# Hybrid encoder block: tile addresses, first norm weights, low parts and opening order

## Chip, cores and metric

One core of a Trainium2 chip (trn2) runs the whole block. The metric is device time in microseconds of one execution; the kernel before took 1340.28 us in the median of three runs (1338.75 to 1340.47).

## What is computed

The reference is one encoder layer on 512 tokens of width 1024, all in float32:

```python
h = rmsnorm(x, g_pre_ffn1)
x = x + 0.5 * rmsnorm(swiglu(h, w_gu1, w_down1), g_post_ffn1)
h = rmsnorm(x, g_pre_mix)
qa, ka, va, qd, kd, vd, ga, gb = split(h @ w_in)
oa = differential_attention(rope(qa), rope(ka), va)   # 8 heads
od = dilated_attention(rope(qd), rope(kd), vd)        # 3 groups of 4 heads
merged = sigmoid(ga) * (oa @ w_proj_a) + sigmoid(gb) * (od @ w_proj_b)
x = x + rmsnorm(merged @ w_out, g_post_mix)
h = rmsnorm(x, g_pre_ffn2)
x = x + 0.5 * rmsnorm(swiglu(h, w_gu2, w_down2), g_post_ffn2)
```

`swiglu` splits `h @ w_gu` into two halves of 2816 columns and returns `(silu(g) * u) @ w_down`.

## The kernel before

**Products in three parts.** Every large float32 operand is split into a high part (a cast to fp32r on ScalarE, L75) and a low part (source minus high part, L76, on VectorE or, where a call names it, on GpSimd). `mm3` (L78 to L81) makes each product of three fp32r matmuls, high by high (L79), high by low (L80) and low by high (L81). Activations lie transposed: `xth`/`xtl` hold the normed input of a stage, `hth`/`htl` the hidden layer of a feed-forward, `odh`/`odl` and `oah`/`oal` the two mixers' outputs, `mh`/`ml` the merged ones.

**Stages.** Feed-forward 1 (`f1`), the mixers, feed-forward 2 (`f2`). In `ffn`, eleven steps of 256 hidden columns make `f1a`/`f2a` from weights (stationary) and `xth`/`xtl` (moving, 512 tokens); the first step does tokens 0 to 255 for all its weights and then tokens 256 to 511. `natural_out` makes the down product with `hth`/`htl` slices as stationary and 512 columns of weights as moving operand, in two halves (`f1dy`, `f1dz`). In its second half the last four weight units are gone through token tile by token tile, and after each tile come the post norm, the residual and the next stage's `pre_norm`, so that the next stage can begin.

**`pre_norm(j, g)`** (L169): two squares with sums on ScalarE, a few 128x1 instructions on VectorE, two `xn` products on VectorE (L179), eight transposes on TensorE (L183), and the split of the result into `xth` (ScalarE) and `xtl` (VectorE).

**Low parts on GpSimd.** The four weight units of the first step of each feed-forward (`f1g`, `f2g` with `fp == 0`, L251), those of `vd0`, the first projection of the mixers (L304), and, left as they are by the change, most query and key units and the first gates.

**Opening** (L792 to L813): 14 warm-up matmuls on the identity, the load of `x` and of three weight units, and `gain(..., on_chip=True)`, which loads one row of 1024 norm weights by ScalarE's queue and spreads it over 128 partitions with a GpSimd instruction (L102). The first `pre_norm` needs it in L179.

**Order.** The framework orders the instructions of every engine itself, by a simulated timeline, from the program order and the dependences; each engine then runs its list in that order.

**Addresses.** Pools are laid one behind the other: `cp` (identity, `xs`, `xth`, `xtl`, norm weights), `wp` (weights), `sp` (small tiles, `xn`, temporaries), then the stage pools (`hp` with `hth`/`htl`; `mp`, `vp`, `op`, `bp`, `dp`). A small tile takes 32 bytes of a partition. By the allocations of this program `cp` and `wp` lie at multiples of 64 bytes (and 128 past a multiple of 256); the odd number of small tiles in `sp` puts `hth`, `htl`, `odh`, `odl`, `oah`, `oal`, `va`, `vd`, the score operands, `xn` and the temporaries 32 bytes past a multiple of 64, and `mh`, `ml`, counted from the other end, as well.

Of the kernel before, what the change touches and what calls it, by code (L numbers as in the profile page):

```python
# [2 lines left out]

# [1 line left out]

# [6 lines left out]
F32 = mybir.dt.float32  # L12
F32R = mybir.dt.float32r
# [5 lines left out]
P = 128  # L19
# [7 lines left out]
ROPE_THETA = 500000.0  # L27
ROT = 16
LAMBDA_INIT = 0.8 - 0.6 * math.exp(-0.3 * 0)
WARM = 14  # L30
SCALE = 1.0 / math.sqrt(64)
NEG = -1e30
C_QA, C_KA, C_VA, C_QD, C_KD, C_VD, C_GA, C_GB = 0, 1024, 2048, 3072, 3840, 4608, 5376, 6400
# [3 lines left out]
def kernel(  # L37
# [8 lines left out]
    nc = tc.nc  # L46
# [4 lines left out]
    w_in = w_in[0]  # L51
# [4 lines left out]
    cp = ctx.enter_context(tc.tile_pool(name="cp", bufs=1))  # L56
    wp = ctx.enter_context(tc.tile_pool(name="wp", bufs=4))
    sp = ctx.enter_context(tc.tile_pool(name="sp", bufs=4))
    ps = ctx.enter_context(tc.tile_pool(name="ps", bufs=4, space=bass.MemoryType.PSUM))

    ident = cp.tile([P, P], F32, name="ident")
    make_identity(nc, ident)
    xs = cp.tile([P, NT, D], F32, name="xs")
# [3 lines left out]
    def psum1(name):  # L67
        return ps.tile([P, 512], F32, tag="p", name=name, bufs=4)
# [4 lines left out]
    def split(hi, lo, src, eng=None):  # L73

        nc.scalar.copy(hi, src)  # L75
        (eng or nc.vector).tensor_tensor(out=lo, in0=src, in1=hi.bitcast(F32), op=ALU.subtract)  # L76
# [11 lines left out]
    def wsplit(raw, a, b, name, eng=None, pool=None):  # L88
        hi = (pool or wp).tile([P, a, b], F32R, tag="wh", name=f"{name}_h")
        lo = (pool or wp).tile([P, a, b], F32R, tag="wl", name=f"{name}_l")  # L90
        split(hi[:], lo[:], raw[:], eng)
        return hi, lo

    def wunit(src, a, b, name, eng=None, pool=None):

        return wsplit(wload(src, a, b, name), a, b, name, eng, pool)

    def gain(g, tag, on_chip=False):
        t = cp.tile([P, D], F32, tag=tag, name=tag)
        if on_chip:  # L100
            nc.scalar.dma_start(t[0:1, :], g)
            nc.gpsimd.partition_broadcast(t[:], t[0:1, :])  # L102
        else:
            nc.sync.dma_start(t[:], g.broadcast_to([P, D]))
        return t

    def small(n, name, dt=F32):
        return sp.tile([P, n], dt, tag=f"{name}{n}", name=name, bufs=1 if name[:2] in ("ys", "pi", "pf", "ld") else 2 if n == 1 else 3)

    def newton(eng, v, r, n):  # L110

# [134 lines left out]
    def ffn_units(w_gu, tag, fp):  # L246

        def block(m, kh):
            c0 = m * FF + fp * 256
            name = f"{tag}g{fp}_{m}{kh}"  # L250
            eng = nc.gpsimd if fp == 0 else None  # L251
            return (lambda: wload(w_gu[kh * 512:(kh + 1) * 512, c0:c0 + 256], 4, 256, name),
                    lambda raw: wsplit(raw, 4, 256, name, eng))
        return [block(m, kh) for m in range(2) for kh in range(2)]

    def ffn(w_gu, w_down, tag, post, after, first=None):
# [23 lines left out]
    def mixers(mix):  # L280
        mp = mix.enter_context(tc.tile_pool(name="mp", bufs=1, reuse_waits="tile"))
# [1 line left out]
        odl = mp.tile([P, 2, S], F32R, name="odl")  # L283
        cosT = mp.tile([P, S], F32, name="cosT")
        sinT = mp.tile([P, S], F32, name="sinT")
        gsub = mp.tile([P, 1], F32, name="gsub")
        nc.sync.dma_start(gsub[:], g_subln.rearrange("a e -> e a"))
        nlam = mp.tile([P, 1], F32, name="nlam")

        def tmp(name, dt=F32):  # L290
            return sp.tile([P, 512], dt, tag="t", name=name, bufs=6)
# [2 lines left out]
        def vproj(c0, cols, put, tag):  # L294
            nu = 8 * cols // 1024
            kk = ND // nu
            us = []

            accs = {}

            def token_half(j, h):
                if not us:
                    us.extend(wunit(w_in[u * kk * P:(u + 1) * kk * P, c0:c0 + cols], kk, cols, f"{tag}{u}",
                                    nc.gpsimd if tag == "vd0" else None) for u in range(nu))  # L304
                if h == 0:
                    accs[j] = psum1(f"{tag}a{j}")
                acc = accs[j]
                for u in range(h * nu // 2, (h + 1) * nu // 2):
                    wh, wl = us[u]
                    for i in range(kk):  # L310
                        k = u * kk + i
                        c = slice(j * P, (j + 1) * P)
                        mm3(acc[:, :cols], xth[:, k, c], xtl[:, k, c], wh[:, i, :], wl[:, i, :], k == 0, k == ND - 1)
                if h == 1:
                    nc.scalar.copy(put(j), acc[:, :cols])
            return [lambda j=j, h=h: token_half(j, h) for j in range(NT) for h in range(2)]


        def rope_tables(bp):
            n = NT * 8  # L320
            scratch = tmp("rt")

            def piece(i):
                return scratch[:, i * n:(i + 1) * n]

            pi = small(NT, "pi", I32)
            nc.sync.dma_start(pi[:], positions.rearrange("b (p j) -> p (b j)", j=NT))
            fr = piece(0)
            nc.sync.dma_start(fr, inv_freq)
            pf = small(NT, "pf")  # L330
            nc.vector.tensor_copy(pf[:], pi[:])
            ang = piece(1)
            nc.vector.tensor_tensor(
                out=ang.rearrange("p (j f) -> p j f", j=NT), in0=fr.rearrange("p (j f) -> p j f", j=NT),
                in1=pf[:].unsqueeze(2).broadcast_to([P, NT, 8]), op=ALU.mult)

            a1 = bp.tile([P, n], F32R, name="a1")
            a2 = piece(2)
            split(a1[:], a2, ang)
            parts, rest = [], 1.0 / (2.0 * math.pi)  # L340
            for _ in range(4):
                e = math.floor(math.log2(rest)) - 11
                b = math.floor(rest / 2.0 ** e) * 2.0 ** e
                parts.append(b)
                rest -= b
            magic = 1.5 * 2.0 ** 23

            def less_round(dst, src):

                t = piece(3)  # L350
                nc.vector.tensor_scalar(t, src, magic, None, op0=ALU.add)
                nc.vector.scalar_tensor_tensor(
                    out=dst, in0=t, scalar=magic, in1=src, op0=ALU.subtract, op1=ALU.subtract)

            u = piece(4)
            nc.vector.memset(u, 0.0)
            for a, m in ((a2, 3), (a1[:].bitcast(F32), 4)):
                for b in reversed(parts[:m]):
                    w = piece(5)
                    nc.vector.tensor_scalar(w, a, b, None, op0=ALU.mult)  # L360
                    less_round(w, w)
                    nc.vector.tensor_tensor(out=u, in0=u, in1=w, op=ALU.subtract)
            for dst, shift in ((sinT, 0.0), (cosT, 0.25)):
                v = piece(6 if shift else 7)
                nc.vector.tensor_scalar(v, u, shift, None, op0=ALU.add)
                less_round(v, v)
                t = piece(8 if shift else 9)
                nc.scalar.activation(t, v, AF.Sin, scale=-6.2831850)
                wide = tmp("wide")
                nc.vector.memset(wide[:], shift * 4.0)  # L370
                wv = wide[:].rearrange("p (j c d) -> p j c d", j=NT, c=2)
                tv = t.rearrange("p (j f) -> p j f", j=NT)
                for c in range(2):
                    if shift == 0.0:
                        nc.vector.tensor_scalar(wv[:, :, c, 0:8], tv, -1.0, None, op0=ALU.mult)
                    else:
                        nc.vector.tensor_copy(wv[:, :, c, 0:8], tv)
# [346 lines left out]
        ep = mix.enter_context(tc.tile_pool(name="ep", bufs=1, side="right", reuse_waits="tile"))  # L724
        mh = [vp.tile([P, 4, S], F32R, tag="v", name="mh0"), ep.tile([P, 4, S], F32R, name="mh1")]
        ml = ep.tile([P, ND, S], F32R, name="ml")

        def pieces(w, c0, nk, a, tag):
            us = [wunit(w[u * 512:min(nk * P, (u + 1) * 512), c0:c0 + 256], min(4, nk), 256, f"{tag}{u}")
# [11 lines left out]
        with tc.tile_pool(name="gp", bufs=1, reuse_waits="tile") as gp:  # L741
# [4 lines left out]
            for cp_ in range(4):  # L746
                c0 = cp_ * 256
# [32 lines left out]
        for j in range(NT):  # L780
            c = slice(j * P, (j + 1) * P)
# [15 lines left out]
    nc.scalar.activation(one[:], one[:], AF.Sqrt)  # L797
    nc.sync.dma_start(xs[:, 0, :], x_v[:, 0, :])
    nc.sync.dma_start(xs[:, 1, :], x_v[:, 1, :])
    g_pre = gain(g_pre_ffn1, "gpre", on_chip=True)  # L800
    steps = ffn_units(w_gu1, "f1", 0)
    raws = [ld() for ld, _ in steps[:3]]
    for j in range(2, NT):
        nc.sync.dma_start(xs[:, j, :], x_v[:, j, :])
    pre_norm(0, g_pre)
    pre_norm(1, g_pre)
    first = [sp_(r) for (_, sp_), r in zip(steps, raws)]
    first.append(steps[3][1](steps[3][0]()))
    pre_norm(2, g_pre)
    pre_norm(3, g_pre)  # L810
    post1 = Post(gain(g_post_ffn1, "gpost"), 0.5)
    g_pre2 = gain(g_pre_mix, "gpre")
    ffn(w_gu1, w_down1, "f1", post1, lambda j: pre_norm(j, g_pre2), first)  # L813
# [48 lines left out]
```

## Time and profile before

| | |
|---|---|
| median of three runs | 1340.28 us |
| the profiled execution | 1340.15 us |
| its span, first to last instruction | 1338.3 us |
| TensorE busy | 1308.1 us (98%) |
| VectorE, ScalarE, GpSimd busy | 611.9, 507.6, 207.9 us |
| mean granted TensorE clock | 0.988 |

The profiled execution lies 0.13 us under the median, with 1.85 us outside its span. TensorE's busy time counts overlapping matmuls once, so the distance from one matmul's start to the next says more than its duration.

### The profile page before, as it was taken

The page shows a single profiled execution, that of the slowest core. Times are in us where ns is not written, and L with a number is a line of the kernel's source. Part 1 is how long each engine was busy: PE and PEld are TensorE (multiplying, and loading weights), DVE is VectorE, ACT ScalarE, POOL GpSimd, SP SyncE. Part 2 cuts the span into 40 slices and gives each one's busy share as a digit, 9 for nine tenths or more (in the row PEclk, how much of TensorE's full clock was granted, in tenths as well). Part 3 has the DMA queues.
Part 4 walks back from the last instruction along what each step waited for, and adds up shares of the span by engine and source line. Part 5 has one row for each costly group of instructions (what it writes and reads, how often), then busy time and mean ns, then how long its engine had stood idle before and what let it go on. Part 6 is the DMA issues. An engine that isn't in the chain of part 4 may idle for free.

```text
span 1338.3 us, 15865 instructions
## 1 busy us (share of the span) xinstructions
PE 1308.1 (98%) x6304; PEld 1077.1 (80%) x6304; DVE 611.9 (46%) x1046; ACT 507.6 (38%) x869; POOL 207.9 (16%) x209
## 2 busy tenths in 40 slices
PE   6999999999999999999999999999999999999997
PEld 6988888888878877887777788888798888888886
DVE  6333333323265265428889944435843232332324
ACT  4332233213145244445776853223432223322221
POOL 3000000000021853018565410000200000000000
PEclk7999999999999999999999999999999999999999
DMA  5323333222233321222111113323223333222221
GB/s 189 111 95 98 104 97 95 95 95 95 95 100 95 96 79 48 64 63 80 48 48 48 53 44 94 102 87 126 79 80 95 100 105 95 95 95 95 95 80 63
DMA packets 111483, 117.63 MB, mean 88 GB/s; under 512 B 4657, under 2 KB 92721, under 8 KB 111410
## 3 DMA queue, kind: packets, MB, share of 16 engines
q1 hardware_dynamic: 111408, 116.62, 27.7%
q8 instruction: 49, 0.80, 0.2%
q14 instruction: 24, 0.20, 0.0%
q10 hardware_dynamic: 2, 0.00, 0.0%
HBM read 114.51 MB, written 2.10 MB: 87 GB/s over the span
## 4 chain that ended last, share of the span: by engine, by line
PE 87%; DVE 7%; ACT 2%; POOL 2%; issue 1%; DMA 1%; SPq 0%; DVEq 0%; POOLq 0%; ACTq 0%
PE f1a L81 6%; PE f1a L80 6%; PE f1a L79 6%; PE f2a L80 6%; PE f2a L81 6%; PE f2a L79 6%; PE f1dy L80 2%; PE f2dy L80 2%; PE f2dz L80 2%; PE f2dz L79 2%; PE f2dy L79 2%; PE f1dy L79 2%; PE f2dz L81 2%; PE f2dy L81 2%; PE f1dy L81 2%; PE f1dz L80 1%
## 5 line engine op out<-in xcount | busy, mean ns | idle before, releaser
L81 PE MATMUL f1a<-xth,f1g_l 128*128 128x512 f32 (+1 forms) x384 | 143.6, 375 | 2.7 <-POOL f1g_l L76 2.7
L80 PE MATMUL f1a<-xtl,f1g_h 128*128 128x512 f32 (+1 forms) x384 | 143.3, 375 | 0.0
L80 PE MATMUL f2a<-xtl,f2g_h 128*128 128x512 f32 (+1 forms) x384 | 143.2, 373 | 0.0
L79 PE MATMUL f1a<-xth,f1g_h 128*128 128x512 f32 (+1 forms) x384 | 143.1, 376 | 0.0
L81 PE MATMUL f2a<-xth,f2g_l 128*128 128x512 f32 (+1 forms) x384 | 143.1, 373 | 0.0
L79 PE MATMUL f2a<-xth,f2g_h 128*128 128x512 f32 (+1 forms) x384 | 142.5, 372 | 0.0
L76 DVE TENSOR_TENSOR f1g_l<-f1g_r,f1g_h 128x1024 fp32r<-128x1024 f32 x40 | 49.0, 1225 | 117.7 <-ACT f1g_h L75 117.7
L76 DVE TENSOR_TENSOR f2g_l<-f2g_r,f2g_h 128x1024 fp32r<-128x1024 f32 x40 | 49.0, 1225 | 117.1 <-ACT f2g_h L75 117.1
L75 ACT CAST f1g_h<-f1g_r 128x1024 fp32r<-128x1024 f32 x44 | 46.2, 1052 | 105.6 <-issue 70.4
L75 ACT CAST f2g_h<-f2g_r 128x1024 fp32r<-128x1024 f32 x44 | 46.3, 1052 | 104.4 <-issue 70.4
L81 PEld LDWEIGHTS f1a<-xth,f1g_l 128*128 128x128 f32 x384 | 73.3, 191 | 15.3 <-POOL f1g_l L76 2.9
L79 PEld LDWEIGHTS f1a<-xth,f1g_h 128*128 128x128 f32 x384 | 73.3, 193 | 12.8 <-ACT xth L75 0.2
L80 PEld LDWEIGHTS f1a<-xtl,f1g_h 128*128 128x128 f32 x384 | 73.5, 192 | 12.4
L81 PEld LDWEIGHTS f2a<-xth,f2g_l 128*128 128x128 f32 x384 | 72.9, 190 | 12.5
L80 PEld LDWEIGHTS f2a<-xtl,f2g_h 128*128 128x128 f32 x384 | 72.9, 190 | 12.4
L79 PEld LDWEIGHTS f2a<-xth,f2g_h 128*128 128x128 f32 x384 | 72.6, 190 | 12.6
L76 DVE TENSOR_TENSOR f1d_l<-f1d_r,f1d_h 128x1024 fp32r<-128x1024 f32 x22 | 27.0, 1226 | 86.3 <-ACT f1d_h L75 86.3
L76 DVE TENSOR_TENSOR f2d_l<-f2d_r,f2d_h 128x1024 fp32r<-128x1024 f32 x22 | 27.0, 1226 | 86.0 <-ACT f2d_h L75 86.0
L76 POOL TENSOR_TENSOR vd_l<-vd_r,vd_h 128x1024 fp32r<-128x1024 f32 x4 | 9.5, 2386 | 357.0 <-ACT vd_h L75 356.9
L75 ACT CAST f1d_h<-f1d_r 128x1024 fp32r<-128x1024 f32 x22 | 23.2, 1053 | 85.1 <-PE f1dy L81 40.9
L75 ACT CAST f2d_h<-f2d_r 128x1024 fp32r<-128x1024 f32 x22 | 23.2, 1053 | 84.8 <-PE f2dy L81 40.9
L636 ACT ACTIVATE ae<-sc,am 128x512 f32<-128x512 f32 x64 | 43.9, 694 | 25.5 <-DVE am L630 25.2
(531 smaller groups left out, 3065.2 us busy)
## 6 DMA issues: line engine op xcount, KB each, us to landing
f1g_r<-in_w_gu_dram SPq DMA_DIRECT2D x44, 512.0 KB, 3.5
f2g_r<-in_w_gu_dram SPq DMA_DIRECT2D x44, 512.0 KB, 3.5
f1d_r<-in_w_down_dram SPq DMA_DIRECT2D x22, 512.0 KB, 3.5
f2d_r<-in_w_down_dram SPq DMA_DIRECT2D x22, 512.0 KB, 3.5
va_r<-in_w_in_dram SPq DMA_DIRECT2D x8, 512.0 KB, 3.6
aq_r<-in_w_in_dram SPq DMA_DIRECT2D x8, 512.0 KB, 3.8
ak_r<-in_w_in_dram SPq DMA_DIRECT2D x8, 512.0 KB, 3.7
ga_r<-in_w_in_dram SPq DMA_DIRECT2D x8, 512.0 KB, 3.8
```

The costliest lines, as they stand in the source:

```text
L75: nc.scalar.copy(hi, src)
L76: (eng or nc.vector).tensor_tensor(out=lo, in0=src, in1=hi.bitcast(F32), op=ALU.subtract)
L79: nc.tensor.matmul(o, ah, bh, start=first, stop=False)
L80: nc.tensor.matmul(o, ah, bl, start=False, stop=False)
L81: nc.tensor.matmul(o, al, bh, start=False, stop=last)
L636: nc.scalar.activation(e[i][:], sc[i][:], AF.Exp, bias=m[:, i:i + 1], accum_out=l[i])
```

## The change

Four things. (1) Small tiles get a pool of their own, `mn`, with fewer buffers for some names, which comes to 64 slots of 32 bytes; `gsub` and `nlam` move into it; three fillers are added (`fill0` of 128 bytes, `a1` of 64 instead of 32 columns, `fill1` of 224 bytes). By the sizes, every tile that TensorE reads then lies at a multiple of 256 bytes, and so of 64. (2) The first norm weights are spread by two float32 matmuls of a row of ones with the loaded row, and copied out of PSUM by ScalarE and VectorE; 9 warm-up matmuls instead of 14. (3) The low parts of the first step of both feed-forwards and of `vd0` go to VectorE. (4) In the opening the split of the first weight unit may be issued only behind the last VectorE and ScalarE instruction of `pre_norm(0)`, and the other splits and `pre_norm(2)`, `pre_norm(3)` behind those of `pre_norm(1)`.

```diff
-WARM = 14
+WARM = 9
...
+    mn = ctx.enter_context(tc.tile_pool(name="mn", bufs=1))
...
+    cp.tile([P, 32], F32, name="fill0")
     ident = cp.tile([P, P], F32, name="ident")
...
             nc.scalar.dma_start(t[0:1, :], g)
-            nc.gpsimd.partition_broadcast(t[:], t[0:1, :])
+            ones = sp.tile([P, 512], F32, tag="t", name="ones", bufs=6)
+            nc.vector.memset(ones[0:1, :P], 1.0)
+            for h in range(2):
+                c = slice(h * 512, (h + 1) * 512)
+                b = psum1(f"gb{h}")
+                nc.tensor.matmul(b[:], ones[0:1, :P], t[0:1, c], start=True, stop=True)
+                if h == 0:
+                    nc.scalar.copy(t[:, c], b[:])
+                else:
+                    nc.vector.tensor_copy(t[:, c], b[:])
...
+    def latest(engine):
+        return next(i for i in reversed(nc.cur_bb.bb.instructions) if i.engine == engine)
+    @contextmanager
+    def behind(*ins):
+        with ExitStack() as st:
+            for i in ins:
+                st.enter_context(tc.issue_after(i))
+            yield
+    def elementwise():
+        return latest(mybir.EngineType.DVE), latest(mybir.EngineType.Activation)
     def small(n, name, dt=F32):
-        return sp.tile([P, n], dt, tag=f"{name}{n}", name=name, bufs=1 if name[:2] in ("ys", "pi", "pf", "ld") else 2 if n == 1 else 3)
+        return mn.tile([P, n], dt, tag=f"{name}{n}", name=name, bufs=1 if name[:2] in ("ys", "pi", "pf", "ld", "ta", "bi") else 2 if n == 1 or name in ("orl", "os", "bv", "bi", "br") else 3)
...
-            eng = nc.gpsimd if fp == 0 else None
...
-                    lambda raw: wsplit(raw, 4, 256, name, eng))
+                    lambda raw: wsplit(raw, 4, 256, name))
...
-                                    nc.gpsimd if tag == "vd0" else None) for u in range(nu))
...
-            a1 = bp.tile([P, n], F32R, name="a1")
+            a1 = bp.tile([P, 64], F32R, name="a1")[:, :n]
...
+        ep.tile([P, 56], F32, name="fill1")
...
+    g_pre = gain(g_pre_ffn1, "gpre", on_chip=True)
     warm = psum1("warm")
...
-    g_pre = gain(g_pre_ffn1, "gpre", on_chip=True)
...
     pre_norm(0, g_pre)
+    at0 = elementwise()
     pre_norm(1, g_pre)
-    first = [sp_(r) for (_, sp_), r in zip(steps, raws)]
-    first.append(steps[3][1](steps[3][0]()))
-    pre_norm(2, g_pre)
-    pre_norm(3, g_pre)
+    at1 = elementwise()
+    with behind(*at0):
+        first = [steps[0][1](raws[0])]
+    with behind(*at1):
+        first += [sp_(r) for (_, sp_), r in zip(steps[1:], raws[1:])]
+        first.append(steps[3][1](steps[3][0]()))
+        pre_norm(2, g_pre)
+        pre_norm(3, g_pre)
```

## Rows read from the trace of the kernel before

**Rows 1.** The page: busy time by engine.

```profile
PE 1308.1 (98%) x6304; PEld 1077.1 (80%) x6304; DVE 611.9 (46%) x1046; ACT 507.6 (38%) x869; POOL 207.9 (16%) x209
```

**Rows 2.** TensorE matmul groups: count, busy us, mean ns of one, idle before.

```profile
L79 PE MATMUL f1a<-xth,f1g_h 128*128 128x512 f32 x320 | 124.5, 389 | 0.0
...
L80 PE MATMUL f1dy<-f1d_l,hth 128*128 128x512 f32 x88 | 35.1, 399 | 0.0
...
L80 PE MATMUL pa<-oal,pa_h 128*128 128x512 f32 x64 | 25.3, 396 | 0.0
...
L79 PE MATMUL wy<-wo_h,mh 128*128 128x512 f32 x64 | 25.1, 395 | 0.0
...
L80 PE MATMUL ga<-xtl,ga_h 128*128 128x512 f32 x64 | 24.9, 390 | 0.0
```

**Rows 3.** Timeline of TensorE in feed-forward 1, up product: start us, us.

```profile
99.66 0.39 PE L79 MATMUL f1a<-xth,f1g_h 128*128 128x512 f32 x1
...
111.90 0.39 PE L79 MATMUL f1a<-xth,f1g_h 128*128 128x512 f32 x1
```

**Rows 4.** Timeline of TensorE in feed-forward 1, down product.

```profile
299.66 0.39 PE L81 MATMUL f1dy<-f1d_h,htl 128*128 128x512 f32 x1
...
311.79 0.39 PE L79 MATMUL f1dy<-f1d_h,hth 128*128 128x512 f32 x1
```

**Rows 5.** Timeline of the opening, all engines.

```profile
1.56 5.57 PE L794 MATMUL warm<-ident 128*128 128x128 f32 x28 [1.56 <-POOL ident masks.py:199]
...
7.72 0.16 DVE L147 TENSOR_TENSOR nr<-rr,nt 128x1 f32<-128x1 f32 x1
...
11.04 1.30 POOL L102 PARTITION_BROADCAST gpre<-gpre  x1 [9.54 <-DMA f1g_r<-in_w_gu_dram]
12.38 1.41 DVE L179 SCALAR_TENSOR_TENSOR xn<-xs,nr,gpre 128x512 f32<-128x512 f32 x2 [4.50 <-POOL gpre L102]
...
17.32 1.23 PE L79 MATMUL f1a<-xth,f1g_h 128*128 128x256 f32 x4
...
19.02 10.04 POOL L76 TENSOR_TENSOR f1g_l<-f1g_r,f1g_h 128x1024 fp32r<-128x1024 f32 x4 [6.68 <-ACT junk L129]
...
21.41 0.58 PE L81 MATMUL f1a<-xth,f1g_l 128*128 128x256 f32 x1 [2.65 <-POOL f1g_l L76]
```

**Rows 6.** DMA queues up to 3 us.

```profile
q10 hardware_dynamic: 2, 0.00, 0.3%
```

**Rows 7.** Stretches of the opening: length, each engine's busy us, granted clock, DMA.

```profile
21.40:26.60 5.20, 5.19 (x24) 5.19 (x25) 5.13 (x5) 1.34 (x2) 5.08 (x3) 0.50 0.62 200
```

**Rows 8.** Timeline between feed-forward 1 and the mixers, TensorE.

```profile
396.14 1.11 PE L183 MATMUL xtp<-ident,xn 128*128 128x128 f32 x4 [3.32 <-DVE xn L179]
```

**Rows 9.** Timeline between the mixers and feed-forward 2, TensorE.

```profile
965.45 1.09 PE L183 MATMUL xtp<-ident,xn 128*128 128x128 f32 x4 [2.12 <-DVE xn L179]
```

**Rows 10.** Windows between feed-forward 1 and the mixers.

```profile
395.30:402.10 6.80, 5.96 (x18) 4.96 (x19) 5.18 (x15) 3.44 (x11) 0.24 (x1) 0.50 0.56 192
```

**Rows 11.** Windows between the mixers and feed-forward 2.

```profile
965.30:968.70 3.40, 3.25 (x16) 3.28 (x17) 2.38 (x8) 1.94 (x5) 0.00 (x0) 0.50 0.75 217
```

**Rows 12.** The page: low parts of a 128x1024 unit by VectorE and by GpSimd.

```profile
L76 DVE TENSOR_TENSOR f1g_l<-f1g_r,f1g_h 128x1024 fp32r<-128x1024 f32 x40 | 49.0, 1225 | 117.7 <-ACT f1g_h L75 117.7
...
L76 POOL TENSOR_TENSOR vd_l<-vd_r,vd_h 128x1024 fp32r<-128x1024 f32 x4 | 9.5, 2386 | 357.0 <-ACT vd_h L75 356.9
```

**Rows 13.** Timeline between feed-forward 1 and the mixers, VectorE.

```profile
388.06 0.21 DVE L140 TENSOR_SCALAR rv<-ss,ssv 128x1 f32<-128x1 f32 x1 [1.41 <-ACT junk L129]
...
391.42 1.76 DVE L147 TENSOR_TENSOR nr<-rr,nt 128x1 f32<-128x1 f32 x1
...
393.23 3.52 DVE L179 SCALAR_TENSOR_TENSOR xn<-xs,nr,gpre 128x512 f32<-128x512 f32 x2
```

**Rows 14.** Timeline between the mixers and feed-forward 2, VectorE.

```profile
956.54 3.03 DVE L208 SCALAR_TENSOR_TENSOR xs<-yg,nr,xs 128x512 f32<-128x512 f32 x2
...
961.80 3.50 DVE L179 SCALAR_TENSOR_TENSOR xn<-xs,nr,gpre 128x512 f32<-128x512 f32 x2
```

More of the change, by code (lines that the diff above doesn't have):

```diff
@@ L1 @@
 import math
-from contextlib import ExitStack
+from contextlib import ExitStack, contextmanager
 import numpy as np
@@ L285, in mixers @@
         sinT = mp.tile([P, S], F32, name="sinT")
-        gsub = mp.tile([P, 1], F32, name="gsub")
+        gsub = mn.tile([P, 1], F32, name="gsub")
         nc.sync.dma_start(gsub[:], g_subln.rearrange("a e -> e a"))
-        nlam = mp.tile([P, 1], F32, name="nlam")
+        nlam = mn.tile([P, 1], F32, name="nlam")
         def tmp(name, dt=F32):
@@ L302, in token_half @@
                 if not us:
-                    us.extend(wunit(w_in[u * kk * P:(u + 1) * kk * P, c0:c0 + cols], kk, cols, f"{tag}{u}",
-                                    nc.gpsimd if tag == "vd0" else None) for u in range(nu))
+                    us.extend(wunit(w_in[u * kk * P:(u + 1) * kk * P, c0:c0 + cols], kk, cols, f"{tag}{u}") for u in range(nu))
                 if h == 0:
@@ L335, in rope_tables @@
                 in1=pf[:].unsqueeze(2).broadcast_to([P, NT, 8]), op=ALU.mult)
-            a1 = bp.tile([P, n], F32R, name="a1")
+            a1 = bp.tile([P, 64], F32R, name="a1")[:, :n]
             a2 = piece(2)
-            split(a1[:], a2, ang)
+            split(a1, a2, ang)
             parts, rest = [], 1.0 / (2.0 * math.pi)
@@ L356, in rope_tables @@
             nc.vector.memset(u, 0.0)
-            for a, m in ((a2, 3), (a1[:].bitcast(F32), 4)):
+            for a, m in ((a2, 3), (a1.bitcast(F32), 4)):
                 for b in reversed(parts[:m]):
```

## The prediction

> **What bounds the kernel now.** The busy table comes first: TensorE is at work for 98% of the span [rows 1], so only two things can shorten the kernel: matmuls that follow each other more closely, and the few stretches in which TensorE waits or runs at its lower clock. The matmul groups are read next, not for their totals but for the mean of one. All groups of rows 2 are the same job, 128x512 in fp32r at the full clock with no wait ahead, yet they fall into two classes: `f1a` and `ga` take 389 to 390 ns, `f1dy`, `pa` and `wy` 395 to 399. Durations overlap, so the timeline gives the pace. In the up product 55 matmuls start between 99.66 and 111.90, that is 54 steps of 226.7 ns [rows 3]. In the down product 53 start between 299.66 and 311.79, 52 steps of 233.3 ns [rows 4]. The difference, 6.6 ns, is not a matter of which operand is stationary or of how often the output bank changes: `pa` has weights as stationary operand and stays in one bank for 24 matmuls, as `ga` does, and is still slow. What the slow groups share is a tile that starts 32 bytes past a multiple of 64 (`hth`, `oal`, `mh`); both operands of the quick groups start on a multiple.
>
> The timeline of the opening and of the two borders between stages shows the rest. At the start, the factor for the first 128 tokens is ready at 7.88 (7.72 + 0.16), but `xn` starts at 12.38, after GpSimd's broadcast of 11.04 to 12.34 [rows 5]. The row it spreads had long landed: ScalarE's queue moved both its packets within the first 3 us [rows 6]. The first feed-forward matmuls start at 17.32 and the stream then stops until the first low part comes from GpSimd at 21.41. From there to 26.6 TensorE is at work without a gap, but at half the granted clock (0.50, 1.2 GHz) [rows 7]. At both borders TensorE waits for `xn`, 3.32 and 2.12 us [rows 8, 9], and has half the clock right after [rows 10, 11].
>
> **The change part by part.**
>
> *Addresses.* The down products are 22 x 4 x 2 x 3 = 528 matmuls in each feed-forward, 1056 in all; 1056 x 6.6 ns = 7.0 us. `pa` (192), `pb` (48) and `wy` (192) are 432 more. By the means of `pa` and `wy` against `ga` [rows 2] each loses 5 to 6 ns, so 2.4 us. Together 9.4 us, all on the path, since TensorE is the bound there and nothing hides it. The bounds: nothing, if the address is not the cause, and 10.5 if the 160 score matmuls gain 6.6 ns too. I take 9.4, because no row shows a score matmul of the quick class. The Trainium skill, page "SBUF — State Buffer", section "Specifications (TRN2)", gives lines of 16 bytes. By that figure a start 32 bytes past a multiple of 64 is as good as any, this term is nothing and the whole sum 13.5. Rows 2 to 4 speak for a coarser step than this, so the measured classes set the term and the rule is a rival below.
>
> *First norm weights.* What goes is the wait of 4.50 us for GpSimd [rows 5]. What comes is two float32 matmuls over 512 columns. A warm-up matmul of 128 columns is two instructions, 28 of which took 5.57 us, 0.2 each [rows 5]; 512 columns are four times that, so 1.6 us each, 3.2 together. Nine warm-ups take 3.6 us. Starting at 1.56, TensorE is through with all of it at 8.4 in whatever order, and a copy of 128x512 takes some 0.7 (half of the pair of 1.41). The weights are thus there between 5.5 (broadcast first) and 9.1, against 7.88 for the factor. `xn` starts at 7.9 to 9.1; I take 8.4, a gain of 4.0. `gain` also moves ahead of the warm-ups and two loads of `x` in the program. Its own load is one row on ScalarE's queue and has landed within 3 us as it is [rows 6]; SP's loads keep their order, and VectorE gets one memset while it is idle.
>
> *Low parts of the opening on VectorE.* From 8.4 VectorE has two pairs of `xn` (2.8), five small instructions of the second tile (0.8), four low parts of 128x512 (half of 1.225 each, 2.4) and the first weight unit's (1.225 [rows 12]): 7.2 us, so the stream can run from 15.6, against 21.41. The gain of the opening is 5.8 with the broadcast's share in it; I take 5.7. ScalarE's cast of that unit, now behind the first tile's, fits between the two tiles' casts. Behind it VectorE has three more low parts (3.7) and the last two `pre_norm`s, about 3.4 each, and is done at 26.1. TensorE's first 96 matmuls last longer than that: 24 at the low clock took 5.2 us [rows 7], and the other 72 at twice that pace 7.8, to 28.6. That cover of 2.5 us is thin; VectorE is what is late next. The clock can move this by 2.6 us either way (half of the 5.2), so the bounds are 2 and 9.
>
> *Feed-forward 1 to mixers.* While GpSimd works on `vd_l`, VectorE's two-input instructions stretch: the pair of `xn` takes 3.52 where 1.41 is normal, a 128x1 product 1.76 instead of 0.16 [rows 5, 13]. Up to the first `xn` half that is 1.6 + 1.05 = 2.65 of the 3.32 us that TensorE waits [rows 8]. VectorE gets four low parts instead, 4 x 1.225 = 4.9 us, where GpSimd needs 2.386 for one [rows 12]. It had idle time ahead (1.41 us before one instruction [rows 13]) in which the first two are due, and the norm comes earlier in the program than the rest. If the wait shrinks to well under 1 us I expect the clock to stay up, as half of the 5.96 us that TensorE was at work at 0.50 is then also saved, 3.0 [rows 10]. Best 6.3, worst a loss of 2.3 (all four ahead of the norm: 4.9 - 2.65). I take 4.5.
>
> *Mixers to feed-forward 2.* Here the residual pair takes 3.03 and the `xn` pair 3.50 instead of 1.41 [rows 14], 3.7 us on the chain that ends in the wait of 2.12 [rows 9]; half the clock for 3.25 busy us costs 1.6 [rows 11]. Best 3.7; nothing if three low parts (3.7) stand ahead of the norm. I take 3.3.
>
> *At nothing:* fewer buffers of small tiles, each used once per head with a whole head's work between; the moved `gsub` and `nlam`; the three fillers; queues, since only the order on VectorE, ScalarE and TensorE changes and the fourth unit's load starts earlier with its buffer.
>
> Sum: 9.4 + 5.7 + 4.5 + 3.3 = 22.9. From the profiled execution's 1340.15, which stands 0.13 under the median, 1317.2; I say 1317.
>
> **The rivals.**
> *The address is not it* (0.10). The slow tiles are also the ones at the high end of the memory, and after the change they stay there. Then the term of 9.4 goes: 1326.6. Against it: six tiles with one thing in common. This is also the outcome by the line figure cited above, which the means of rows 2 do not bear out.
> *The borders only change hands* (0.12). VectorE, now with the low parts, makes TensorE wait as long at both borders, and the opening gains 2: 1340.15 - 9.4 - 2 = 1328.7. For it: the worst cases above. Against it: `xn` alone gets back 2.1 us at each.
> *A slower kernel* (0.03). The quick tiles lie 128 bytes past a multiple of 256 and move too; all end on multiples of 256, where no row shows any tile. If that start were as slow as the 32-byte offset, 3744 quick matmuls (3264 of 512 columns, 480 of 256) would lose 6.6 ns, 24.7 us, and the 9.4 would not come: 1317.2 + 34.1 = 1351. It decides as soon as `f1a` steps at more than 230 ns.
> *A much faster one* (0.03), for the same reason turned round: 512 columns at 2.4 GHz are 213.3 ns, so a step of 226.7 has 13.4 ns to lose; over some 5200 matmuls 70 us, 1247.
>
> **How the numbers follow.** The forecast holds 0.72 and by its bounds reaches from 1307 to 1325. The range goes on to 1329 for the first two rivals and leaves the last two out. A measurement of this kernel tells 0.2%, 2.7 us, from no change. Faster by more than that is 0.93: the forecast, both first rivals less a little, and the last; slower 0.04 and same 0.03 come from the third and from the worst cases added up.
>
> **What would show it.** Right: `f1dy`, `pa` and `wy` at 389 to 390 ns and steps near 227; no broadcast on GpSimd; first `xn` near 8.4 and the matmul stream from about 15.6; no four low parts on GpSimd at the borders, `xn` pairs of 1.4, waits there under 1 us and no window at 0.50. Wrong: down steps still at 233, or `f1a` off 227; a new wait of TensorE for a VectorE low part or for `xtl` at a border; half the clock past 26 us.

## The result and the profile after

The changed kernel takes 1319.15 us (median of 4 runs, 1317.87 to 1319.91) where the kernel before, beside it on the same chip, took 1340.38: a ratio of 0.9843, 95% interval 0.9826 to 0.9860, so 18.8 to 23.3 us less. The profiled span fell from 1338.3 to 1317.5.

The page's busy line of the changed kernel, and behind it its matmul groups (count, busy us, mean ns of one, idle before), answer [rows 1, 2]:

```profile
PE 1296.0 (98%) x6298; PEld 1070.7 (81%) x6298; DVE 604.9 (46%) x1060; ACT 507.7 (39%) x870; POOL 177.8 (13%) x196
```

```profile
L83 PE MATMUL f1a<-xth,f1g_h 128*128 128x512 f32 x320 | 124.5, 389 | 0.0
...
L83 PE MATMUL f1dy<-f1d_h,hth 128*128 128x512 f32 x88 | 34.2, 389 | 0.0
L84 PE MATMUL f1dy<-f1d_l,hth 128*128 128x512 f32 x88 | 34.2, 389 | 0.0
...
L84 PE MATMUL ga<-xtl,ga_h 128*128 128x512 f32 x64 | 24.9, 390 | 0.0
L84 PE MATMUL pa<-oal,pa_h 128*128 128x512 f32 x64 | 24.9, 389 | 0.0
L83 PE MATMUL wy<-wo_h,mh 128*128 128x512 f32 x64 | 24.8, 389 | 0.0
```

The slow class of [rows 2] is gone: `f1dy`, `pa` and `wy` stand at 389 with `f1a` and `ga`. In the timeline the down product answers [rows 4] with 54 starts, 53 steps of 226.6 ns in place of 233.3:

```profile
294.34 0.39 PE L84 MATMUL f1dy<-f1d_l,hth 128*128 128x512 f32 x1
...
306.35 0.39 PE L83 MATMUL f1dy<-f1d_h,hth 128*128 128x512 f32 x1
```

The opening, all engines, against [rows 5, 7]: the norm weights go through TensorE at 2.46, the first half of `xn` starts at 7.67 in place of 12.38, and the stream of matmuls runs from 15.88 in place of 21.41. The second block is the windows view (length; busy us of TensorE, its weight loads, VectorE, ScalarE and GpSimd; granted clock; DMA share and GB/s): the granted clock is 0.50 (1.2 GHz, called the half clock below) for 3.4 us of the opening, where before it was so from 9.6 to 26.7.

```profile
2.46 3.75 PE L111 MATMUL gb<-gpre,ones 1*128 1x512 f32 x4 [2.46 <-DMA gpre<-in_g_pre_ffn_dram]
...
7.67 0.75 DVE L207 SCALAR_TENSOR_TENSOR xn<-xs,nr,gpre 128x512 f32<-128x512 f32 x1
...
8.68 0.67 DVE L115 COPY gpre<-gb 128x512 f32<-128x512 f32 x1
9.39 0.75 DVE L207 SCALAR_TENSOR_TENSOR xn<-xs,nr,gpre 128x512 f32<-128x512 f32 x1
...
13.93 1.22 DVE L80 TENSOR_TENSOR f1g_l<-f1g_r,f1g_h 128x1024 fp32r<-128x1024 f32 x1
...
15.88 0.58 PE L84 MATMUL f1a<-xtl,f1g_h 128*128 128x256 f32 x1 [1.24 <-DVE xtl L80]
```

```profile
15.30:18.70 3.40, 2.83 (x13) 2.83 (x14) 3.40 (x6) 3.26 (x9) 0.00 (x0) 0.50 0.53 157
```

Between feed-forward 1 and the mixers (SyncE's queue, VectorE, TensorE), against [rows 8, 13]:

```profile
377.00 1.23 DVE L80 TENSOR_TENSOR vd_l<-vd_r,vd_h 128x1024 fp32r<-128x1024 f32 x1 [0.24 <-ACT vd_h L79]
...
381.26 0.43 SPq L355 DMA_DIRECT2D rt<-in_inv_freq_dram  x1
...
387.07 0.19 DVE L359 TENSOR_TENSOR rt<-rt,pf 128x32 f32<-128x32 f32 x1 [2.03 <-DMA rt<-in_inv_freq_dram]
...
387.25 1.40 DVE L207 SCALAR_TENSOR_TENSOR xn<-xs,nr,gpre 128x512 f32<-128x512 f32 x2
...
388.04 1.32 PE L211 MATMUL xtp<-ident,xn 128*128 128x128 f32 x8 [1.59 <-DVE xn L207]
...
390.91 0.50 PE L85 MATMUL vd0a<-vd_h,xtl 128*128 128x512 f32 x1 [0.80 <-DVE xtl L80]
...
393.83 0.23 DVE L417 TENSOR_TENSOR lq<-lq 128x64 f32<-128x64 f32 x1 [1.74 <-DMA lq<-in_lambda_k_dram]
...
398.93 0.50 PE L83 MATMUL vd0a<-vd_h,xth 128*128 128x512 f32 x1 [1.17 <-ACT xth L79]
```

The `xn` pair is back at 1.40 from 3.52, and yet TensorE still waits for it: VectorE stands 2.03 us for the load of `inv_freq`, with `xn` queued behind, and later 1.74 us for `lambda_k`. Between the mixers and feed-forward 2 nothing of the kind is left (VectorE and TensorE, against [rows 9, 14]); TensorE has a single wait there, of 0.24 us:

```profile
945.23 1.41 DVE L236 SCALAR_TENSOR_TENSOR xs<-yg,nr,xs 128x512 f32<-128x512 f32 x2
...
949.27 1.41 DVE L207 SCALAR_TENSOR_TENSOR xn<-xs,nr,gpre 128x512 f32<-128x512 f32 x2
...
960.96 0.74 PE L83 MATMUL f2a<-xth,f2g_h 128*128 128x256 f32 x4 [0.24 <-ACT xth L79]
```

Where the 20.8 us of span came from is worked out from the starts of the same matmuls in each trace. The columns are: *opening*, to the last `f1a`; *down 1*, from the first `f1dy` to the last `f1dz`; *border 1*, from there to the first `vd1a`; *products*, from the last `ao` to the last `wy`; *border 2*, from there to the last `f2a`; *down 2*, from there to the last `f2dz`; and the stretches at a granted clock of 0.50, but for the one at the very end. From `vd1a` to `ao` all kernels take 379.6 to 379.8.

| kernel | opening | down 1 | border 1 | products | border 2 | down 2 | half clock at |
|---|---|---|---|---|---|---|---|
| before | 265.36 | 123.84 | 33.41 | 157.70 | 247.16 | 123.21 | 9.6-26.7, 395.3-402.1, 965.3-968.7 |
| after | 259.88 | 120.35 | 31.87 | 155.00 | 243.15 | 119.68 | 15.3-18.7 |
| addr_only | 266.38 | 120.37 | 33.17 | 155.00 | 245.92 | 119.68 | 9.8-26.9, 405.8-409.2 |
| only64 | 260.02 | 120.35 | 31.87 | 155.99 | 243.13 | 119.68 | 16.8-20.2 |
| offsets | 258.42 | 123.82 | 31.42 | 155.00 | 243.15 | 123.17 | none |
| early_loads | 260.10 | 123.35 | 31.81 | 157.17 | 243.16 | 122.71 | 16.4-19.8, 409.0-412.4 |
| all_at_32 | 261.27 | 120.35 | 33.33 | 155.00 | 243.15 | 119.68 | 15.1-21.9, 390.5-397.3 |
| offset_256 | 260.05 | 120.35 | 32.05 | 155.00 | 243.15 | 120.89 | 15.6-19.0 |
| early2 | 258.22 | 120.35 | 28.74 | 155.00 | 243.15 | 119.68 | none |
| vd_gpsimd | 258.38 | 120.35 | 32.54 | 155.00 | 243.15 | 119.68 | 386.4-389.8 |
| f2_gpsimd | 258.26 | 120.35 | 31.77 | 155.00 | 248.34 | 119.68 | 949.3-956.1 |
| broadcast_gpsimd | 261.77 | 120.37 | 31.61 | 155.00 | 243.15 | 119.68 | none |
| free_order | 259.45 | 120.35 | 33.57 | 155.00 | 243.15 | 119.68 | 14.4-17.8, 400.1-403.5 |
| f1_gpsimd | 259.73 | 120.36 | 33.63 | 155.00 | 243.15 | 119.68 | 17.6-21.0, 389.7-396.5 |

After minus before: opening 5.5, down products 3.5 twice, border 1 1.5, products 2.7, border 2 4.0, together 20.7.

### The profile page after: what moved, and what is told of

Same layout as the page of the kernel before. It is cut to its first block, busy times and chain, and to the rows that moved or that the text cites. A ratio compares the mean times of both kernels' runs of the same rounds, so it can differ in the third digit from the quotient of the medians.

```text
span 1317.5 us, 15855 instructions
## 1 busy us (share of the span) xinstructions
PE 1296.0 (98%) x6298; PEld 1070.7 (81%) x6298; DVE 604.9 (46%) x1060; ACT 507.7 (39%) x870; POOL 177.8 (13%) x196
## 4 chain that ended last, share of the span: by engine, by line
PE 89%; DVE 6%; POOL 2%; ACT 1%; issue 1%; DMA 1%; DVEq 0%; SPq 0%; POOLq 0%
PE f1a L84 6%; PE f1a L85 6%; PE f2a L83 6%; PE f2a L84 6%; PE f1a L83 6%; PE f2a L85 6%; PE f2dz L85 2%; PE f1dz L83 2%; PE f1dz L84 2%; PE f2dy L85 2%; PE f2dy L83 2%; PE f1dy L84 2%; PE f2dz L83 2%; PE f1dy L85 2%; PE f1dz L85 2%; PE f1dy L83 2%
## 5 line engine op out<-in xcount | busy, mean ns | idle before, releaser
L80 DVE TENSOR_TENSOR f2g_l<-f2g_r,f2g_h 128x1024 fp32r<-128x1024 f32 x44 | 53.9, 1225 | 117.7 <-ACT f2g_h L79 117.7
L80 DVE TENSOR_TENSOR f1g_l<-f1g_r,f1g_h 128x1024 fp32r<-128x1024 f32 x44 | 53.8, 1225 | 117.4 <-ACT f1g_h L79 117.4
L80 POOL TENSOR_TENSOR dq_l<-dq_r,dq_h 128x1024 fp32r<-128x1024 f32 x6 | 14.8, 2470 | 415.7 <-DVE vd_l L80 411.0
```

## The experiments

**Addresses alone on the kernel before** (addr_only):

```diff
+    mn = ctx.enter_context(tc.tile_pool(name="mn", bufs=1))
...
+    cp.tile([P, 32], F32, name="fill0")
...
-        return sp.tile([P, n], dt, tag=f"{name}{n}", ...
+        return mn.tile([P, n], dt, tag=f"{name}{n}", ...
...
+        ep.tile([P, 56], F32, name="fill1")
```

> The kernel before with the tile addresses of the change and nothing else of it. Theory (the address is the whole cause of the slow matmul class): f1dy, pa and wy go from steps of 233 to 227 ns, the three places give 7.0 + 1.6 + 1.1 = 9.7 us and the time is about 1330.6, ratio 0.993; the opening and both borders stay as before. Rival (part of it comes from the new order of the low parts): clearly under 9 us here, steps between 227 and 233.

Measured: 1332.62 against 1338.92, ratio 0.9948 (0.9928 to 0.9967), that is 4.4 to 9.6 us; the span fell by 10.2. The table shows where: 3.5 + 3.5 + 2.7 us in the three products, 9.7 by the trace where the prediction had 9.4; the opening takes 1.0 more than before, and the borders 0.2 and 1.2 less. So by the trace the address part is worth what the classes of [rows 2] said, and the rest of the change the other half. The median fell by less, 6.3: the five runs reach from 1328.98 to 1335.03, with mean granted clocks from 0.992 to 0.987, and the traced one is among the two quickest.

**Multiples of 64 only** (only64: the changed kernel without its first filler, with `a1` back at 32 columns and a smaller last filler, which puts most operands at 128 past a multiple of 256 and `mh1` and `ml` at 192):

```diff
-    cp.tile([P, 32], F32, name="fill0")
...
-            a1 = bp.tile([P, 64], F32R, name="a1")[:, :n]
+            a1 = bp.tile([P, 32], F32R, name="a1")[:, :n]
...
-        ep.tile([P, 56], F32, name="fill1")
+        ep.tile([P, 8], F32, name="fill1")
```

> The changed kernel without the fillers: its tiles lie at multiples of 64 bytes, most of them 128 past a multiple of 256. Theory (a multiple of 64 is enough): within 1 us of the changed kernel, 1319, f1dy steps of 226.7 ns. Rival (256 is what counts): f1dy, pa and wy go back to steps of 233 and the time to about 1329.

Measured: 1320.29, ratio 0.9857 (0.9842 to 0.9871). All as in the changed kernel, except `wy`, which is slow again (products 155.99 in place of 155.00) though every one of its tiles starts at a multiple of 64. Neither theory had that.

```profile
L83 PE MATMUL wy<-wo_l,mh 128*128 128x512 f32 x64 | 25.4, 397 | 0.0
```

**Other offsets of `hth` and `htl`** (offsets: by the allocations 16 and 112 bytes in feed-forward 1, 4 and 96 in feed-forward 2):

```diff
-            hth = hp.tile([P, NF, S], F32R, name="hth")
-            htl = hp.tile([P, NF, S], F32R, name="htl")
+            oh, ol = (4, 12) if tag == "f1" else (1, 8)
+            hth = hp.tile([P, NF * S + 16], F32R, name="hth")[:, oh:oh + NF * S]...
+            htl = hp.tile([P, NF * S + 16], F32R, name="htl")[:, ol:ol + NF * S]...
```

> The changed kernel with hth and htl shifted inside their pool: by 16 and 48 bytes in feed-forward 1, by 4 and 32 in feed-forward 2. Theory (what counts is whether a row of the stationary tile starts on a multiple of 64): all four slow, down steps of 233 in both feed-forwards, 7 us more than the changed kernel, about 1326. Rival (finer lines: 32 or 16 bytes): the one at 32 bytes is quick in feed-forward 2, or 16, 32 and 48 all are, and less than 3 us is lost. Second rival (the cost grows with the offset): the four products of the down step differ by their tile's offset.

Measured: 1326.02, ratio 0.9903 (0.9885 to 0.9921); both down products back at 3.5 us more, 53 steps of 233.2 ns in the timeline, as much in feed-forward 2 as in feed-forward 1. The edit also lengthened `hth` by 64 bytes, so that `htl`, behind it, moved by 64 more than the 48 and 32 that the expectation names; 96 is still a multiple of 32, as its rival asks. The Trainium skill, page "SBUF — State Buffer", section "Specifications (TRN2)", gives lines of 16 bytes. The offsets of 16, 96 and 112 bytes are multiples of that and slow here, so that line is not what decides.

```profile
L83 PE MATMUL f1dy<-f1d_h,hth 128*128 128x512 f32 x88 | 34.9, 397 | 0.0
```

**The small loads of the mixers early** (early_loads: `inv_freq` and lambda, with its arithmetic, moved into feed-forward 1):

```diff
-    cp.tile([P, 32], F32, name="fill0")
...
             for fp in range(NF // 2):
+                if mid and fp == 3:
+                    mid()
...
+    fr_t = mn.tile([P, 32], F32, name="fr")
...
+    def early():
+        nc.sync.dma_start(fr_t[:, 0:32], inv_freq)
+        lambda_value()
...
```

> The changed kernel with the table of frequencies loaded and the lambda value computed in feed-forward 1, so that no VectorE instruction at the border to the mixers waits for those loads. Theory (the missing 3 us of the border are VectorE's list standing still for two loads, 2.0 and 1.7 us, with xn behind them): TensorE's waits for xn there go from 1.6 and 0.3 and what follows them to under 0.5 in all, 2 to 3.5 us less than the changed kernel, about 1316.5. Rival (the four low parts on VectorE are what delays xn): the waits stay and the time is within 1 us of 1319.

Measured: 1328.17, ratio 0.9918 (0.9903 to 0.9933), 9 us slower than the changed kernel, and for a reason that had nothing to do with the loads: without the first filler the weights and `xth` start at 128 past a multiple of 256, `hth`, `htl` and `oah` at 0, and the down products, `pa`, `pb` and half of `wy` are slow. Every tile that TensorE reads is at a multiple of 128 here. One of its groups, and its timeline with 52 steps of 232.5 ns:

```profile
L82 PE MATMUL f1dy<-f1d_h,hth 128*128 128x512 f32 x88 | 34.7, 395 | 0.0
```

```profile
294.26 0.40 PE L84 MATMUL f1dy<-f1d_h,htl 128*128 128x512 f32 x1
...
306.35 0.39 PE L82 MATMUL f1dy<-f1d_h,hth 128*128 128x512 f32 x1
...
408.04 0.50 PE L82 MATMUL vd0a<-vd_h,xth 128*128 128x512 f32 x1 [1.82 <-ACT xth L78]
```

Border 1 was no shorter (31.81), but differently made: the third token block of `vd0` was through 21.3 us after the last `f1dz`, 3.1 earlier than in the changed kernel (24.4). Then ScalarE took the two sines of the angle tables, with a table load of 1.28, ahead of the last `xth` cast, TensorE waited 1.82 (last line), and the clock fell to 0.50 at 409.0.

Together with only64 this gave a new theory: what counts is not where a tile starts but the **distance between the two operands of a matmul** within 256 bytes. The groups of the 389-ns class in the kernel before had both operands at 128 past a multiple of 256; those of the 395-ns class had one operand there and the other elsewhere, or two elsewhere that differ, but for 32 of the 192 matmuls of `wy`, which stand alike between slow ones. `wy` of early_loads speaks for it within one trace: by the allocations its first 49 matmuls, but for one, have operands 128 bytes apart and step at 232.6 ns; the next 47 have both on a multiple of 256, and from the sixth of them on the steps are 227.3:

```profile
906.69 0.40 PE L82 MATMUL wy<-wo_h,mh 128*128 128x512 f32 x1
...
917.85 0.39 PE L84 MATMUL wy<-wo_h,ml 128*128 128x512 f32 x1
...
919.24 0.39 PE L84 MATMUL wy<-wo_h,ml 128*128 128x512 f32 x1
...
928.56 0.39 PE L84 MATMUL wy<-wo_h,ml 128*128 128x512 f32 x1
```

**Everything moved by 32 bytes** (all_at_32):

```diff
-    cp.tile([P, 32], F32, name="fill0")
+    cp.tile([P, 40], F32, name="fill0")
...
-        ep.tile([P, 56], F32, name="fill1")
+        ep.tile([P, 48], F32, name="fill1")
```

> The changed kernel with everything in SBUF moved by 32 bytes (first filling tile 160 bytes in place of 128, the other 192 in place of 224): every operand of TensorE then starts at 32 past a multiple of 256, and every pair of operands keeps the same distance. Theory 'distance' (formed from the run with early loads, whose tiles were all at multiples of 128 and whose down products were slow all the same, and from the run 'multiples of 64 only', whose last product alone was slow): a matmul is quick when its two operands stand at the same place within 256 bytes, wherever that is. Then all 128x512 steps stay at 226.5 to 227 ns and the time is that of the changed kernel, 1319 us, within 1.5. Theory 'multiples of 64' (that of the change): no operand is at one, so f1a and f2a fall to 233.3 ns as well: (1920 + 1056) x 6.6 ns + 2.4 us = 22 us more, 1341 us.

Measured: 1320.82, ratio 0.9851 (0.9836 to 0.9867). No operand is at a multiple of 64, and all are quick; timeline of `f1a` and `f1dy`, 54 steps of 226.7 ns each:

```profile
99.66 0.39 PE L83 MATMUL f1a<-xth,f1g_h 128*128 128x512 f32 x1
...
111.90 0.39 PE L83 MATMUL f1a<-xth,f1g_h 128*128 128x512 f32 x1
...
294.14 0.39 PE L83 MATMUL f1dy<-f1d_h,hth 128*128 128x512 f32 x1
...
306.38 0.39 PE L83 MATMUL f1dy<-f1d_h,hth 128*128 128x512 f32 x1
```

"Multiples of 64" falls by 20 us. The profiled execution was 2.9 us longer than that of the changed kernel, all of it in the opening and border 1, where it had the half clock for longer; the instructions are the same.

**The period of the distance** (offset_256; as in only64 without the first filler, the last one here of 96 bytes):

```diff
-    cp.tile([P, 32], F32, name="fill0")
...
-            hth = hp.tile([P, NF, S], F32R, name="hth")
+            oh = 64 if tag == "f1" else 48
+            hth = hp.tile([P, NF * S + 64], F32R, name="hth")[:, oh:oh + NF * S]...
...
-        ep.tile([P, 56], F32, name="fill1")
+        ep.tile([P, 24], F32, name="fill1")
```

> The changed kernel with its tiles at 128 past a multiple of 256, hth of feed-forward 1 moved by 256 bytes against the weights and htl of both feed-forwards too, hth of feed-forward 2 by 192. It asks for the period of the distance. Period 256 (or less): the down products of feed-forward 1 stay at 226.7 ns, in feed-forward 2 the 352 with hth fall to 232 to 233 and the 176 with htl don't: 352 x 6.6 ns = 2.3 us over the changed kernel, 1321.5 us. Period 512 or more: all 1056 are slow and half of wy: 7.0 + 0.6 us, 1326.8 us. Period 64: all stay quick, 1319 us.

Measured: 1320.5, ratio 0.9849 (0.9835 to 0.9862). Feed-forward 1, with a distance of 256, is quick: 53 steps of 226.8 ns. Feed-forward 2 (`hth` at 192, `htl` at 256) takes 228.9 ns a step and 1.2 us more in all, half of the 2.3 expected:

```profile
294.27 0.39 PE L82 MATMUL f1dy<-f1d_h,hth 128*128 128x512 f32 x1
...
306.29 0.39 PE L84 MATMUL f1dy<-f1d_h,htl 128*128 128x512 f32 x1
...
1224.66 0.39 PE L83 MATMUL f2dy<-f2d_l,hth 128*128 128x512 f32 x1
...
1236.79 0.39 PE L82 MATMUL f2dy<-f2d_h,hth 128*128 128x512 f32 x1
```

So 0 and 256 are alike, and 64 (only64), 128 (early_loads), 192 and the offsets of 4, 16, 96 and 112 are slow, by sizes that differ.

**The loads early, with addresses kept** (early2: the moves of early_loads, but with `fr_t` in the filler's place and the sines behind the last `xth` cast of feed-forward 1):

```diff
-    cp.tile([P, 32], F32, name="fill0")
+    fr_t = cp.tile([P, 32], F32, name="fr")
...
-                nc.scalar.activation(t, v, AF.Sin, scale=-6.2831850)
+                with behind(at2):
+                    nc.scalar.activation(t, v, AF.Sin, scale=-6.2831850)
...
+    at2 = latest(mybir.EngineType.Activation)
```

> The changed kernel with the loads of inv_freq and of the lambdas, and the arithmetic of lambda, moved into feed-forward 1 (fourth pair of columns), inv_freq in the place of the filling tile so that all addresses stay, and with the two sines of the angle tables put behind the last xth cast of feed-forward 1 on ScalarE. Theory 'loads' (what is left of the border from feed-forward 1 to the mixers is VectorE's 2.03 us for inv_freq and 1.74 us for lambda_k): in the run with early loads the third token block of vd0 ended 3.1 us earlier after the last f1dz, then ScalarE's sines took 1.5 of it and a clock drop 1.7; with the sines behind, 1.4 to 3.1 us of the border are gained: from the last f1dz to the first vd1 28.8 to 30.5 us in place of 31.9, time 1316 to 1317.7 us. Rival 'norm chain': the xn, xtp, xth, xtl chain of each token sets the border whatever is loaded when: 31.9 us, time 1319 us.

Measured: 1316.36, ratio 0.9824 (0.9811 to 0.9837). Border 1 takes 28.74, 3.1 less than in the changed kernel. VectorE and TensorE there:

```profile
383.67 1.40 DVE L207 SCALAR_TENSOR_TENSOR xn<-xs,nr,gpre 128x512 f32<-128x512 f32 x2
...
386.08 0.50 PE L83 MATMUL vd0a<-vd_h,xth 128*128 128x512 f32 x1 [0.28 <-ACT xth L79]
...
387.48 0.50 PE L85 MATMUL vd0a<-vd_h,xtl 128*128 128x512 f32 x1 [0.67 <-DVE xtl L80]
```

`xn` starts 4.9 us after the last `f1dz` (378.80) where it was 6.8 (380.46 to 387.25), and TensorE no longer waits for it. Theory "loads" holds, "norm chain" falls. By its median this is also the fastest kernel of the study, 2.8 us below the changed one; the two ratios' intervals overlap, so it is the trace that carries this.

**Low parts of `vd0` back on GpSimd** (vd_gpsimd):

```diff
-   us.extend(wunit(..., f"{tag}{u}") for u in range(nu))
+   us.extend(wunit(..., f"{tag}{u}", nc.gpsimd if tag == "vd0" else None) for u in range(nu))
```

> The changed kernel with the four low parts of vd0 given back to GpSimd (the 2.4-us operations of before). Theory 'they pay' (1.5 us gained at this border are theirs): last f1dz to first vd1 back at 33.4 us, with the clock drop of before, 1320.7 us. Rival 'they take VectorE's time and pay nothing there, the gain is the order of loads': no change or faster by up to 1 us, 1318 to 1319 us.

Measured: 1320.1, ratio 0.9849 (0.9833 to 0.9865), not to be told from the changed kernel. GpSimd, VectorE and TensorE in the timeline, and the windows view:

```profile
375.54 9.64 POOL L80 TENSOR_TENSOR vd_l<-vd_r,vd_h 128x1024 fp32r<-128x1024 f32 x4 [374.24 <-ACT vd_h L79]
...
382.84 3.56 DVE L207 SCALAR_TENSOR_TENSOR xn<-xs,nr,gpre 128x512 f32<-128x512 f32 x2
...
385.79 0.66 PE L211 MATMUL xtp<-ident,xn 128*128 128x128 f32 x4 [3.50 <-DVE xn L207]
```

```profile
386.40:389.80 3.40, 3.40 (x12) 2.71 (x11) 2.96 (x10) 2.15 (x6) 0.00 (x0) 0.50 0.55 190
```

The stretch of [rows 13], the wait of [rows 8] and the half clock are all back, and border 1 is only 0.7 us longer. TensorE's waits of over 0.15 us in border 1 add up to 4.9 us here, one of them 3.5; in the changed kernel they are six, 4.4 in all. Kernels with the changed one's instructions at border 1 take 33.3 to 33.6 there when the clock falls to 0.50 (all_at_32, free_order, f1_gpsimd) and 31.4 to 32.1 when it doesn't. The 32.54 of this run lies between, so neither theory is shown, and what the move alone is worth as long as the loads are late stays open.

**Low parts of feed-forward 2's first units back on GpSimd** (f2_gpsimd):

```diff
-                    lambda raw: wsplit(raw, 4, 256, name))
+                    lambda raw: wsplit(raw, 4, 256, name, nc.gpsimd if fp == 0 and tag == "f2" else None))
```

> The changed kernel with the four low parts of feed-forward 2's first units given back to GpSimd. Theory 'shared stretch' (the gain of 4.0 us from the last wy to the last f2a came from taking GpSimd's low parts off VectorE's norm there): the xn and residual pairs are at 3.0 to 3.5 us again in place of 1.41, TensorE waits some 2 us for xn and has half the clock once: last wy to last f2a 3 to 4 us longer, 1322 to 1323 us. Rival 'addresses and spreading order brought it': the pairs stay near 1.4 us and the time at 1319 us.

Measured: 1324.09, ratio 0.9878 (0.9864 to 0.9891), 4.9 us over the changed kernel; border 2 is 5.2 longer. VectorE and TensorE:

```profile
941.79 3.02 DVE L236 SCALAR_TENSOR_TENSOR xs<-yg,nr,xs 128x512 f32<-128x512 f32 x2
...
947.05 3.50 DVE L207 SCALAR_TENSOR_TENSOR xn<-xs,nr,gpre 128x512 f32<-128x512 f32 x2
...
950.70 1.09 PE L211 MATMUL xtp<-ident,xn 128*128 128x128 f32 x4 [2.12 <-DVE xn L207]
```

These are [rows 9, 14] to within a hundredth. It is a little more than expected: TensorE also waited 1.02 us for an `xn` half before that, and the half clock lasted 6.8 us in place of the 3.4 of [rows 11].

**The three parts of the opening, one undone at a time.** The broadcast on GpSimd again:

```diff
-            ones = sp.tile(...)
...
-                nc.tensor.matmul(b[:], ones[0:1, :P], t[0:1, c], start=True, stop=True)
+            nc.gpsimd.partition_broadcast(t[:], t[0:1, :])
```

> The changed kernel with the first norm weights spread by GpSimd's partition broadcast, all else as changed. Theory: the wait for it (xn at 12.4 in place of 7.7 us) is most of the opening's gain of 5.5 us; the matmul stream then starts 3.5 to 4.7 us later than 15.9, last f1a 3 to 5 us later, 1322 to 1324 us. Rival: GpSimd, freed from the low parts, has the broadcast done early and nothing is lost: 1319 us.

no written order:

```diff
-    with behind(*at0):
-    with behind(*at1):
+    with ExitStack():
+    with ExitStack():
```

> The changed kernel without the written order of its opening instructions (the two places that hold the casts, the low parts and the third and fourth tile's norm behind the first two tiles' on VectorE and ScalarE). Theory 'the order matters': VectorE and ScalarE take weight units and later tiles between the first two tiles' norm, the first f1a starts after 14.1 and the stream after 15.9 us, 1 to 3 us later: 1320 to 1322 us. Rival 'the planner finds it by itself': 1319 us.

the low parts of the first four units on GpSimd:

```diff
-                    lambda raw: wsplit(raw, 4, 256, name))
+                    lambda raw: wsplit(raw, 4, 256, name, nc.gpsimd if fp == 0 and tag == "f1" else None))
```

> The changed kernel with the low parts of the first four weight units of feed-forward 1 given back to GpSimd (2.4 to 2.5 us each, one after the other). Theory: the first unit's low part comes by 14 us and the stream starts as early as now, but each next unit comes 2.4 us later while 24 matmuls of 256 columns take 2.8 us at the full clock, and xn and xtl on VectorE stretch meanwhile: 1 to 3 us lost, 1320 to 1322 us. Rival 'low parts set the opening': the stream waits for each of the four, 4 to 5 us lost, 1323 to 1324 us. Rival 'no matter': 1319 us.

Measured: 1323.32 (0.9871, 0.9858 to 0.9885), 1320.32 (0.9849, 0.9836 to 0.9863) and 1320.91 (0.9851, 0.9837 to 0.9864). Of the kernel with the broadcast on GpSimd, GpSimd, VectorE and TensorE:

```profile
11.53 1.30 POOL L106 PARTITION_BROADCAST gpre<-gpre  x1 [10.02 <-issue]
12.86 1.42 DVE L198 SCALAR_TENSOR_TENSOR xn<-xs,nr,gpre 128x512 f32<-128x512 f32 x2 [5.18 <-POOL gpre L106]
...
19.61 0.39 PE L84 MATMUL f1a<-xtl,f1g_h 128*128 128x256 f32 x1 [1.30 <-DVE xtl L80]
```

GpSimd had nothing else to do and still comes to the broadcast only at 11.53. Without any half clock its opening takes 261.77, against 258.2 to 258.4 in the four kernels with the changed opening and as little half clock: 3.5 us. The other two have 3.4 us of half clock and take 259.45 and 259.73, against 259.9 to 260.1 in the four kernels with the changed opening and the same: no loss at all. Their medians, 1.2 and 1.8 us over the changed kernel, lie in the ranges of the theories, but for another reason: what the traces have more lies in border 1, under a half clock there, and is within what the measurement tells. What both together would cost was not tried.

## Why the prediction was right, and where not

*Addresses, 9.4:* 9.7 in the table, 3.5 twice and 2.7; addr_only shows them alone. The step "what the slow groups share is a tile that starts 32 bytes past a multiple of 64" gave the right list of matmuls for a wrong reason: all_at_32 is quick with every operand off a multiple of 64, early_loads slow with every tile on one. What they share is a partner at another place within 256 bytes. That also says why no score matmul gained: `mak` and `maq` stood at the same place before and after, and their mean went from 430 to 429 ns. The number came right by luck: the change put all operands on multiples of 256, and so all pairs at the same place, and there both rules forecast the same.

*Opening, 5.7:* 5.5. The 4.0 for the broadcast measured 3.5 alone. The 1.7 for the low parts is not shown to be theirs: undone alone they cost nothing. The rest of the gain goes with the clock, at 0.50 from 9.6 to 26.7 before and for 0 to 6.8 us after, in whichever kernel; the same instructions took 258.2 to 261.3. What ended the long half clock, and whether it needs the low parts, the order or the earlier start, was not taken apart, so that the sum came out at 5.5 is in part luck.

*Feed-forward 1 to mixers, 4.5:* 1.5, the mis-sized term. The step that failed is "I take 4.5": it gave back the stretch of `xn` and the half clock and asked what low parts stand ahead of the norm, but not which loads do. VectorE, earlier than before, came to the product with `inv_freq`, which in the kernel before stood behind that `xn` ([rows 13] and the line below), and waited 2.03 us for a row issued behind two weight units and a mask; lambda's row came next.

```profile
396.73 0.18 DVE L333 TENSOR_TENSOR rt<-rt,pf 128x32 f32<-128x32 f32 x1
```

One of the prediction's own signs of being wrong came with it: TensorE waits 0.80 us for `xtl` there. Nor is the 1.5 safe: the border had the half clock before and not after, and with it the same instructions take 33.3 to 33.6 (all_at_32, free_order, f1_gpsimd), as long as the 33.41 of before. With the loads out of the way, and no half clock, the border is 4.7 shorter than before (33.41 to 28.74), about the forecast size. How much of that is the low parts' is not shown, since no run has the loads early and the low parts on GpSimd.

*Mixers to feed-forward 2, 3.3:* 4.0, and f2_gpsimd takes it away. The low parts on VectorE cost nothing visible there: TensorE has no wait but the 0.24.

The rivals: "the address is not it" falls with addr_only, and by region too, since `hth` and `htl` moved by 32 bytes only and their products are now at 389. "The borders only change hands" holds for border 1 in part, not for border 2. "Slower" and "much faster" fall with `f1a`, still at 389 ns (226.7 a step) on multiples of 256. The forecast's bounds, 1307 to 1325, do not follow from those of its terms: the best cases add up to 29.5 us, 1310.7, and the worst to no gain.

## What to carry to other kernels

When equal matmuls fall into two classes by their mean, write down the start of both operands and compare them with each other, not each with a round number; a filler that moves one pool against another can cost as much as it brings. When an engine gets faster ahead of a norm or any other chain, look for the next thing in its own queue that waits for a transfer, and issue that transfer a stage earlier. And before a low part or a cast is moved off GpSimd, look at which two-input VectorE instructions lie under it: that is where it costs.

## What was not expected of the hardware

- 128x512 matmuls in fp32r step at 226.6 to 226.8 ns when the two operands are 0 or 256 bytes apart (as far as tried), at whatever place, and at 232.5 to 233.3 ns when they are 4 and 96 (offsets), 16 and 112 (offsets), 128 (early_loads) apart, or, in the kernel before, 96 with the stationary tile the lower of the two. They are in the slow class at 64 too (`wy` of only64). At 192, where two of three matmuls have that distance, the mean step is 228.9, half the loss. A mechanism was not looked for.
- The half clock comes and goes in the same instruction stream: all_at_32 had it from 390.5 to 397.3, the changed kernel, whose instructions are the same, not at all there. Border 1 was 33.33 and 31.87. A border's gain of 1.5 us in one trace is thus not safe by itself.
- GpSimd, idle, started a broadcast at 11.53 whose row had long landed and for which the timeline names no waiting but its own issue.
